# Four pairs of k-tiles by seven products, quarters on GpSimd's queue, and a transposition inside SBUF, in a hybrid decoder block

## The chip, the cores and the metric

The kernel runs on one core of a Trainium2 chip. The metric is the device time of one execution in microseconds, as a median over runs; three runs of the kernel before are shown. Engines: PE multiplies matrices and writes to PSUM, DVE (VectorE) and ACT (ScalarE) work elementwise, POOL (GpSimd) does little here but issue DMAs, SP (SyncE) only issues DMAs. Each engine takes its own instructions in order and waits for others by semaphores.

## The reference, cut to what matters

```python
D_MODEL, SEQ, D_FF = 2048, 256, 5632

def swiglu(x, w_gu, w_down):
    gate, up = jnp.split(x @ w_gu, 2, axis=-1)
    return (jax.nn.silu(gate) * up) @ w_down

def reference(x, p, ...):
    h = x
    h = h + 0.5 * swiglu(rms_norm(h, ffn1_norm), ffn1_w_gu, ffn1_w_down)
    h = h + hybrid_mixer(rms_norm(h, mix_norm), ...)      # w_in, DeltaNet + stick-breaking, w_out
    h = h + 0.5 * swiglu(rms_norm(h, ffn2_norm), ffn2_w_gu, ffn2_w_down)
    gate = jax.nn.sigmoid(rms_norm(h, ple_norm) @ ple_w_gate)
    h = h + gate * (p @ ple_w_proj)
    return rms_norm(h, final_norm)
```

Everything is float32. x has 256 rows and 2048 columns. The change is in the two feed-forward networks (FFN1 and FFN2) and, a little, in the last stage with the gate.

## The kernel before, in words

**Three products for one.** A float32 operand is cut into a high part (type fp32r) and the rest (also fp32r): x = xh + xl, w = wh + wl. A product is xh·wh + xh·wl + xl·wh, three matmuls, each with a stationary 128x128 tile of activations and a moving 128x512 tile of weights. For weights the cut is made on chip. `weight_pair` (L62) takes two k-tiles (128x1024 elements, a *pair*): SP loads them into `raw` (4 buffers, L64), ACT casts `whi` (L72), DVE subtracts `wlo` (L73); `whi` and `wlo` have 3 buffers each. One pair used as it is (*plain*) serves both halves of the 256 rows: 2 k-tiles x 2 halves x 3 = 12 matmuls (L480 to L482).

**Seven products for eight.** A *group* works on two blocks of 512 columns (b = 0, 1) at once and holds four banks of PSUM (two halves of rows x two blocks). For its first `NS` pairs of k-tiles it uses Strassen's scheme in Winograd's form: pair g is a 2x2 block matrix on either side (two k-tiles by two halves of rows; two k-tiles by two blocks of columns), and seven products of sums stand for eight. NS is 3 in the gate-and-up groups, and `NS_DOWN` is 3 or 2 in the down groups. The sums of weights are made from four *quarters* (k-tile j, block b) of NS x 512 columns: tiles `R`, four tags, loaded in `Group.load` (L270). `all_sums` (L276) yields seven sums in the order (0,0), (0,0), (0,0), (0,1), (1,0), (0,0), (1,1): each is the quarter as it stands then, cast on ACT to `shi` (L284) and subtracted on DVE to `slo` (L285), 2 buffers each. After the first sum DVE adds a quarter to another (L289) and GpSimd issues a load from DRAM that adds to a quarter (L293); after the second DVE adds once more; after the third another accumulating load. `product(i)` (L306) does 3 x NS matmuls for sum i; after products 2 and 3 DVE adds banks to banks (L324), by way of a copy on ACT (L323).

**Sums of activations.** `halves` (L393) makes the four sums on the other side, `Sh` and `Sl`: it adds high and low parts (L405), makes four sums (L412), casts (L413) and subtracts (L414), two pairs at a time.

**Stages.** Each FFN has 11 gate-and-up (gu) groups in three parts of 3, 4 and 4, and after each part two down (dn) groups of its hidden blocks. FFN1 starts with two gu groups without sums, FFN2 with one. When the last plain pair of a gu group is through, `down_input` (L433) multiplies silu(gate) by up (L435) and transposes the 256x512 result: DVE transposes 32x32 blocks (L167), SP writes them to DRAM (L171) and reads them back in another order (L181; the helper is `transposed`), then ACT and DVE cut them into `hTh` and `hTl` (L443, L444). `halves` for the dn groups runs at the start of a part's last gu group, `halves` for the next part's gu groups at the start of its second dn group.

**Order.** `plan` (L333) writes the order by hand: between the plain pairs of a group stand the seven products of the next one (*seventh*), from place `first` on, one after each plain pair. The quarters of the group after that are issued on SP from the fifth of these places on. `next_weights` keeps two to three pairs and up to two sums prepared ahead. Side work (transposes, `halves`, the mixer's chains) stands in generators in `lanes`; one step of each lane follows each plain pair. The list so written is then put in its final order on each engine by the program's scheduler, so rows of different kinds may change places.

**Elsewhere.** The mixer (stage between the FFNs) and the last stage use plain pairs alone, through `accumulate`. The last stage multiplies by `w_pg` and, in `embed`, by `w_pp`.

Of the kernel before, what the change touches and what calls it, by code (L numbers as in the profile page):

```python
# [10 lines left out]
F32 = mybir.dt.float32  # L11
# [18 lines left out]
NS = 3  # L30
NS_DOWN = tuple(3 if i1 - i0 == 4 else 2 for i0, i1 in PARTS)
# [10 lines left out]
def block_kernel(ctx, tc, a, out):  # L42
# [156 lines left out]
    def norm_block(nT, which, j, tmp):  # L199

        if j < 3:
            lanes.add(0, norm_block_behind(nT, which, j, tmp))
            return
# [39 lines left out]
    class Group:  # L243
# [24 lines left out]
        def load(self, j, b):  # L268

            self.raw[j, b] = raw = current[0].tile([P, NS, NB], F32, tag=f"R{j}{b}", name="R")[:, 0:self.ns]  # L270
            nc.sync.dma_start(out=raw, in_=self.quarters[b][j])
# [61 lines left out]
    def plan(n):  # L333
# [24 lines left out]
        made = []  # L358
        for i, group in enumerate(groups):
# [3 lines left out]
            at, loads = [], {}  # L363
# [25 lines left out]
    for nb in range(3):  # L389
        order += [("pair", a["w_pp"][nb])] + [("pair", a["w_pg"][nb][g]) for g in range(KD // 2)]  # L390
    order.append(("pair", a["w_pp"][3]))

    def halves(kind, his, los, ns, wait=0):  # L393
# [5 lines left out]
        sh = fp.tile([P, 4, NS, P], F32R, tag="Sh", name="Sh")  # L399
        sl = fp.tile([P, 4, NS, P], F32R, tag="Sl", name="Sl")  # L400
        for g0 in range(0, ns, 2):
            n = min(2, ns - g0)
            hi, lo = his[g0 // 2], los[g0 // 2]
            x = fp.tile([P, 2, 4, P], F32, tag="tT", name="tT").rearrange("p t q y -> p (t q y)")[:, 0:2 * n * T]
            nc.vector.tensor_tensor(out=x, in0=hi[:, 0:2 * n].bitcast(F32).rearrange("p k x -> p (k x)"),  # L405
                                    in1=lo[:, 0:2 * n].bitcast(F32).rearrange("p k x -> p (k x)"), op=ALU.add)
            x = x.rearrange("p (g j t y) -> p g j t y", g=n, j=2, t=2)
            a11, a12, a21, a22 = (x[:, :, j, t, :] for t in range(2) for j in range(2))
            s = fp.tile([P, 4, 2, P], F32, tag="S", name="S")[:, :, 0:n]
            for o, y, z, op in ((0, a21, a22, ALU.subtract), (1, s[:, 0], a11, ALU.subtract),  # L410
                                (2, a21, a11, ALU.subtract), (3, s[:, 1], a12, ALU.add)):
                nc.vector.tensor_tensor(out=s[:, o], in0=y, in1=z, op=op)  # L412
            nc.scalar.copy(sh[:, :, g0:g0 + n], s)  # L413
            nc.vector.tensor_tensor(out=sl[:, :, g0:g0 + n], in0=s, in1=sh[:, :, g0:g0 + n], op=ALU.subtract)  # L414
            yield

        def side(i, g):
            if i in (0, 4, 5):
                k, t = 2 * (g % 2) + (i > 0), i // 5
                c = slice(t * P, (t + 1) * P)  # L420
                return his[g // 2][:, k, c], los[g // 2][:, k, c]
            x = {1: 0, 2: 1, 3: 2, 6: 3}[i]
            return sh[:, x, g, :], sl[:, x, g, :]

        sides[kind] = side

    def ffn(n, nT, r, scale, next_norm, stat):
        xs = picker(*nT)
        late = callable(r)
        with tc.tile_pool(name="ffn", bufs=1) as fp:  # L430
            hTh, hTl = [], []

            def down_input(u, sil, th, tl):  # L433
# [4 lines left out]
                tT = fp.tile([P, 2, 4, P], F32, tag="tT", name="tT")  # L438
                yield from transposed(lambda t: sil[:, t, :], tT)
                for t in range(2):  # L440
                    hi, lo = (x[:, :, t * P:(t + 1) * P].rearrange("p j (q y) -> p q j y", q=4) for x in (th, tl))
                    tv = tT[:, t].rearrange("p q (j y) -> p q j y", j=4)
# [12 lines left out]
            for group, todo in ffn_plan[n]:  # L455
# [11 lines left out]
                for kind, one in todo:  # L467
# [19 lines left out]
                    if dn:  # L487
# [7 lines left out]
                        if group.last:  # L495
                            norm_block(nxt, next_norm, nb, lambda: fp.tile([P, 2, 4, P], F32, tag="tT", name="tT"))
                            lanes.advance(0)
# [3 lines left out]
                    else:  # L501
# [8 lines left out]
                        gen = down_input(outs, sil, th, tl)  # L510
# [58 lines left out]

    pp = ctx.enter_context(tc.tile_pool(name="pp", bufs=1))  # L570
    pT = act.tile([P, 2, T], F32, tag="nat", name="pT", bufs=4)
    nc.sync.dma_start(out=pT, in_=a["pT"])
    ph = pp.tile([P, 2, T], F32R, tag="ph", name="ph")
    pl = pp.tile([P, 2, T], F32R, tag="pl", name="pl")
    nc.scalar.copy(ph, pT)
    nc.vector.tensor_tensor(out=pl, in0=pT, in1=ph, op=ALU.subtract)
# [4 lines left out]
    with tc.tile_pool(name="fin", bufs=1) as fp:  # L581
        fg = fp.tile([P, D], F32, tag="fg", name="fg")
        nc.scalar.dma_start(out=fg, in_=a["final_norm"].broadcast_to([P, D]))
        stat = new_stat()
# [18 lines left out]
        for nb in range(3):  # L603
            e = embed(nb)
            gt = [mm_ps("gt") for _ in range(2)]
            accumulate(gt, xs, KD)
            for t in range(2):
# [671 lines left out]
```

## Time and profile before

| what | value |
|---|---|
| median of three runs | 1961.52 us (1959.1 to 1963.86) |
| the profiled execution | 1958.5 us, of which the span is 1956.8 us |
| granted TensorE clock | 0.998 |
| VectorE busy | 1536.0 us, 78% |
| ScalarE busy | 1153.7 us, 59% |
| GpSimd busy | 83.9 us, 4% |
| DMA | 468.28 MB, mean 239 GB/s |

The span runs from the first to the last instruction; the profiled execution's time is 1.7 us longer. FFN1 lies between 8 and 697 us, the mixer between 698 and 1159 us, FFN2 up to 1847 us, the last stage after that. A stretch of 40 us is about one group. Matmul ends are modelled, so a matmul's listed length (389 ns) is more than the distance from one to the next; the pace is read from a stretch of known count. A row of groups reads: line, engine, operation, out<-in, shape, count, then busy time and mean ns of one, then the engine's idle time just before them and what ended it.

### The profile page before, as it was taken

What the parts mean: (1) busy time and instruction counts of PE and PEld (TensorE: products, weight loads), DVE (VectorE), ACT (ScalarE), POOL (GpSimd) and SP (SyncE); (2) the same over time, 40 slices, a digit from 0 to 9 for tenths busy, and PEclk for the clock granted to TensorE, in tenths of its full rate; (3) what the DMA queues carried; (4) which work ended last, traced back from release to release, by engine and by line L of the source; (5) the groups of instructions that cost most, each with busy time, mean ns of one, the idle gap of its engine ahead of it and who ended that gap; (6) DMA issues with size and microseconds to landing.
All of it is one profiled execution on the core that took longest, in us unless ns stands there. A gap on an engine that the chain in (4) does not pass through costs nothing.

```text
span 1956.8 us, 24735 instructions
## 1 busy us (share of the span) xinstructions
PE 1939.7 (99%) x8945; PEld 1606.5 (82%) x8945; DVE 1536.0 (78%) x1771; ACT 1153.7 (59%) x1402; POOL 83.9 (4%) x108
## 2 busy tenths in 40 slices
PE   9999999999999999999999999999999999999998
PEld 7887888888888888878788888888888888888887
DVE  6889778897788766797856678888879887798755
ACT  7655656566565567664555465665566555665554
POOL 0000000000000000010100000000000000000000
PEclk9999999999999999999999999999999999999999
DMA  8988888888888765556555788887888878887764
GB/s 316 296 238 255 265 275 243 261 257 260 264 254 256 222 209 165 174 169 213 178 195 160 243 289 243 253 270 242 250 265 281 281 223 247 261 271 239 236 207 147
DMA packets 164379, 468.28 MB, mean 239 GB/s; under 512 B 20641, under 2 KB 59553, under 8 KB 164129
## 3 DMA queue, kind: packets, MB, share of 16 engines
q1 hardware_dynamic: 154176, 418.57, 62.1%
q0 software_dynamic: 8928, 46.67, 13.6%
q8 instruction: 70, 1.15, 0.2%
q10 hardware_dynamic: 1152, 1.47, 0.2%
q14 instruction: 53, 0.43, 0.1%
HBM read 444.62 MB, written 22.02 MB: 238 GB/s over the span
## 4 chain that ended last, share of the span: by engine, by line
PE 90%; DVE 5%; issue 3%; DMA 1%; ACT 1%; POOL 0%; SPq 0%; ACTq 0%; POOLq 0%; DVEq 0%
PE u L481 6%; PE u L482 6%; PE u L480 5%; PE g L480 5%; PE g L482 5%; PE g L481 5%; PE d L480 5%; PE d L482 5%; PE d L481 5%; PE pj L108 3%; PE pj L109 3%; PE pj L107 3%; PE g L316 3%; PE g L318 3%; PE g L317 3%
## 5 line engine op out<-in xcount | busy, mean ns | idle before, releaser
L72 ACT CAST whi<-raw 128x1024 fp32r<-128x1024 f32 (+1 forms) x531 | 557.0, 1051 | 525.3 <-PE d L482 113.6
L73 DVE TENSOR_TENSOR wlo<-raw,whi 128x1024 fp32r<-128x1024 f32 (+1 forms) x531 | 643.2, 1216 | 217.9 <-ACT whi L72 212.5
L285 DVE TENSOR_TENSOR slo<-R,shi 128x1536 fp32r<-128x1536 f32 (+1 forms) x217 | 365.6, 1686 | 125.1 <-ACT shi L284 123.5
L284 ACT CAST shi<-R 128x1536 fp32r<-128x1536 f32 (+1 forms) x217 | 309.7, 1428 | 158.6 <-PE g L318 50.6
L481 PE MATMUL u<-wlo,nTh 128*128 128x512 f32 x476 | 185.3, 389 | 0.2 <-DVE wlo L73 0.2
L481 PE MATMUL g<-wlo,nTh 128*128 128x512 f32 x476 | 185.4, 390 | 0.0
L482 PE MATMUL g<-whi,nTl 128*128 128x512 f32 x476 | 185.3, 389 | 0.0
L482 PE MATMUL u<-whi,nTl 128*128 128x512 f32 x476 | 185.2, 389 | 0.0
L480 PE MATMUL u<-whi,nTh 128*128 128x512 f32 x476 | 184.9, 389 | 0.0
L480 PE MATMUL g<-whi,nTh 128*128 128x512 f32 x476 | 184.3, 389 | 0.3 <-ACT whi L72 0.3
L107 PE MATMUL pj<-whi,nTh 128*128 128x512 f32 x448 | 179.6, 401 | 0.0
L108 PE MATMUL pj<-wlo,nTh 128*128 128x512 f32 x448 | 175.3, 391 | 2.2 <-DVE wlo L73 2.2
L109 PE MATMUL pj<-whi,nTl 128*128 128x512 f32 x448 | 174.9, 390 | 0.0
L481 PE MATMUL d<-wlo,hTh 128*128 128x512 f32 x448 | 174.3, 389 | 0.0
L480 PE MATMUL d<-whi,hTh 128*128 128x512 f32 x448 | 174.3, 389 | 0.0
L482 PE MATMUL d<-whi,hTl 128*128 128x512 f32 x448 | 174.3, 389 | 0.0
L289 DVE TENSOR_TENSOR R<-R 128x1536 f32<-128x1536 f32 (+1 forms) x62 | 104.4, 1684 | 0.9
L481 PEld LDWEIGHTS u<-wlo,nTh 128*128 128x128 f32 x476 | 89.3, 188 | 19.1 <-DVE wlo L73 0.7
L481 PEld LDWEIGHTS g<-wlo,nTh 128*128 128x128 f32 x476 | 89.4, 188 | 19.0 <-DVE wlo L73 0.4
L480 PEld LDWEIGHTS g<-whi,nTh 128*128 128x128 f32 x476 | 89.3, 188 | 18.9 <-ACT whi L72 0.5
L482 PEld LDWEIGHTS u<-whi,nTl 128*128 128x128 f32 x476 | 89.4, 188 | 18.6
L480 PEld LDWEIGHTS u<-whi,nTh 128*128 128x128 f32 x476 | 89.3, 188 | 18.6
(304 smaller groups left out, 3223.8 us busy)
## 6 DMA issues: line engine op xcount, KB each, us to landing
raw<-in_w_gu SPq DMA_DIRECT2D x237, 512.0 KB, 5.5
raw<-in_w_down SPq DMA_DIRECT2D x112, 512.0 KB, 5.2
raw<-in_w_in SPq DMA_DIRECT2D x112, 512.0 KB, 3.5
R<-in_w_gu2q SPq DMA_DIRECT2D x40, 768.0 KB, 5.9
R<-in_w_gu1q SPq DMA_DIRECT2D x36, 768.0 KB, 5.9
scr<-tb SPq DMA_DIRECT2D x74, 256.0 KB, 4.8
raw<-in_w_out SPq DMA_DIRECT2D x32, 512.0 KB, 4.6
raw<-in_w_pg SPq DMA_DIRECT2D x32, 512.0 KB, 4.1
```

The lines of the kernel that those rows point to most:

```text
L72: nc.scalar.copy(hi[:, j, :], raw[:, j, :])
L73: nc.vector.tensor_tensor(out=lo[:, j, :], in0=raw[:, j, :], in1=hi[:, j, :], op=ALU.subtract)
L107: nc.tensor.matmul(outs[t], xh[:, c], whi[:, j, :], start=st, stop=False)
L108: nc.tensor.matmul(outs[t], xh[:, c], wlo[:, j, :], start=False, stop=False)
L109: nc.tensor.matmul(outs[t], xl[:, c], whi[:, j, :], start=False, stop=sp)
L284: nc.scalar.copy(hi, w)
L285: nc.vector.tensor_tensor(out=lo, in0=w, in1=hi, op=ALU.subtract)
L289: nc.vector.tensor_tensor(out=self.raw[x], in0=self.raw[x], in1=self.raw[y], op=ALU.add)
L316: nc.tensor.matmul(out, xh, whi[:, g, :], start=st, stop=False, skip_group_check=True)
L480: nc.tensor.matmul(out, xh[:, c], whi[:, j, :], start=st, stop=False, skip_group_check=True)
L481: nc.tensor.matmul(out, xh[:, c], wlo[:, j, :], start=False, stop=False, skip_group_check=True)
L482: nc.tensor.matmul(out, xl[:, c], whi[:, j, :], start=False, stop=sp, skip_group_check=True)
```

## The change

Seven parts:

- `NS` goes from 3 to 4, and `NS_DOWN` from 3 to 4 in the parts of four blocks. The quarters, `shi`, `slo`, `Sh` and `Sl` grow by a third.
- `raw` has three buffers in place of four.
- The quarters of all but the first group with sums are issued by GpSimd, in the order (0,0), (0,1), (1,1), (1,0); each takes the buffer that the group before frees next (`home`). The fourth is carried over into the next group.
- The seven products follow each other from place 1, 2 or 8 on, one after each plain pair.
- `down_input` no longer goes through DRAM: sixteen DMAs, each 32 partitions by 1 KB, carry the blocks from SBUF to SBUF; the high and low parts are made three or four steps later.
- `halves` makes its four sums in place, in the tile `sil` which it shares with `down_input`.
- Norm blocks alternate between two lanes and two tiles; `embed` comes behind the eight pairs of `w_pg`, and p is cut in the last stage.

```diff
-NS = 3
-NS_DOWN = tuple(3 if i1 - i0 == 4 else 2 for i0, i1 in PARTS)
+NS = 4
+NS_DOWN = tuple(4 if i1 - i0 == 4 else 2 for i0, i1 in PARTS)
...
-        raw = wp.tile([P, 2, NB], F32, tag="raw", name="raw", bufs=4)
+        raw = wp.tile([P, 2, NB], F32, tag="raw", name="raw", bufs=3)
...
-            self.raw[j, b] = raw = current[0].tile([P, NS, NB], F32, tag=f"R{j}{b}", name="R")[:, 0:self.ns]
-            nc.sync.dma_start(out=raw, in_=self.quarters[b][j])
-
-        def loads(self):
-            return [("load", lambda j=j, b=b: self.load(j, b)) for j, b in ((0, 1), (1, 0), (0, 0), (1, 1))]
+            self.raw[j, b] = raw = current[0].tile([P, NS, NB], F32, tag=self.home[j, b], name="R")[:, 0:self.ns]
+            self.queue.dma_start(out=raw, in_=self.quarters[b][j])
+
+        def loads(self, last=None):
+            free = [last.home[q] for q in ((0, 1), (1, 0), (0, 0), (1, 1))] if last else ["R0", "R1", "R2", "R3"]
+            self.queue = nc.gpsimd if last else nc.sync
+            use = (0, 0), (0, 1), (1, 1), (1, 0)
+            self.home = dict(zip(use, free))
+            return [("load", lambda q=q: self.load(*q)) for q in use]
...
-                first = 2 if group.ns else 8
-                at = [first + j * (n_plain - 1 - first) // 7 for j in range(7)]
+                first = 8 if not group.ns else 1 if group.kind == follower.kind else 2
+                at = [min(first + j, n_plain - 1) for j in range(7)]
...
-                    for x, one in zip((5, 6, 7, 7), after.loads()):
-                        loads.setdefault(at[x] if x < 7 else min(at[6] + 1, n_plain - 1), []).append(one)
+                    *three, last = after.loads(follower)
+                    for x, one in zip((4, 5, 6), three):
+                        loads.setdefault(at[x], []).append(one)
+                    carried = [last]
...
-        order += [("pair", a["w_pp"][nb])] + [("pair", a["w_pg"][nb][g]) for g in range(KD // 2)]
+        order += [("pair", a["w_pg"][nb][g]) for g in range(KD // 2)] + [("pair", a["w_pp"][nb])]
...
+            x = fp.tile([P, 2 * NB], F32, tag="sil", name="S")[:, 0:n * NB]
...
+            for o, y, z, op in ((a22, a21, a22, ALU.subtract), (a21, a21, a11, ALU.subtract),
+                                (a11, a22, a11, ALU.subtract), (a12, a11, a12, ALU.add)):
+                nc.vector.tensor_tensor(out=o, in0=y, in1=z, op=op)
...
-                tT = fp.tile([P, 2, 4, P], F32, tag="tT", name="tT")
-                yield from transposed(lambda t: sil[:, t, :], tT)
+                tb = fp.tile([P, 4, 2, P], F32, tag="tb", name="tb")
+                for t in range(2):
+                    nc.vector.transpose(tb[:, :, t].rearrange("p c (j x) -> p c j x", j=4),
+                                        sil[:, t, :].rearrange("p (j c x) -> p c j x", j=4, c=4))
+                yield
+                tT = fp.tile([P, 4, 2, P], F32, tag="tT", name="tT")
+                for c in range(4):
+                    for q in range(4):
+                        nc.sync.dma_start(out=tT[32 * c:32 * c + 32, q], in_=tb[32 * q:32 * q + 32, c])
+                    if c == 1 and wait > 3:
+                        yield
+                for _ in range(wait):
+                    yield
```

Three places show how the order moves. The first is DVE at the start of a gu group in the second part of FFN1; `slo` is a sum, `R` a quarter, `tb` the transposed blocks. Before:

```order
L285 TENSOR_TENSOR slo_2142<-R_2061,shi_2141 128x1536
L289 TENSOR_TENSOR R_2061<-R_2061,R_2020 128x1536
L73 TENSOR_TENSOR wlo_2106<-raw_2104,whi_2105 128x1024
L285 TENSOR_TENSOR slo_2172<-R_2061,shi_2171 128x1536
L435 SCALAR_TENSOR_TENSOR sil_1961<-u0_1623,rstd2_517,sil_1961 128x512
L435 SCALAR_TENSOR_TENSOR sil_1961<-u1_1624,rstd2_517,sil_1961 128x512
L73 TENSOR_TENSOR wlo_2137<-raw_2135,whi_2136 128x1024
L167 STREAM_TRANSPOSE tb_2161<-sil_1961 128x512
L167 STREAM_TRANSPOSE tb_2162<-sil_1961 128x512
L73 TENSOR_TENSOR wlo_2167<-raw_2165,whi_2166 128x1024
L289 TENSOR_TENSOR R_2061<-R_2061,R_2063 128x1536
```

The same place in the change:

```order
L291 TENSOR_TENSOR slo_2118<-R_1999,shi_2117 128x2048
L445 SCALAR_TENSOR_TENSOR sil_1974<-u0_1633,rstd2_515,sil_1974 128x512
L295 TENSOR_TENSOR R_1999<-R_1999,R_2041 128x2048
L445 SCALAR_TENSOR_TENSOR sil_1974<-u1_1634,rstd2_515,sil_1974 128x512
L73 TENSOR_TENSOR wlo_2141<-raw_2139,whi_2140 128x1024
L451 STREAM_TRANSPOSE tb_2174<-sil_1974 128x4x128
L291 TENSOR_TENSOR slo_2158<-R_1999,shi_2157 128x2048
L451 STREAM_TRANSPOSE tb_2174<-sil_1974 128x4x128
L295 TENSOR_TENSOR R_1999<-R_1999,R_2077 128x2048
```

The two additions of quarters now have one plain pair's `wlo` between them, where three stood, and both they and the sums are a third longer.

The second place is PE in the last gu group of the same part, where the products of the first dn group (banks d) stand between plain pairs (banks g and u). Before:

```order
L316 MATMUL d0_2878<-shi_2826,Sh_2809 128x512
L317 MATMUL d0_2878<-slo_2827,Sh_2809 128x512
L318 MATMUL d0_2878<-shi_2826,Sl_2810 128x512
L480 MATMUL g0_2534<-whi_2855,nTh_102 128x512
L481 MATMUL g0_2534<-wlo_2856,nTh_102 128x512
L482 MATMUL g0_2534<-whi_2855,nTl_106 128x512
L480 MATMUL g1_2535<-whi_2855,nTh_102 128x512
```

The same place in the change:

```order
L504 MATMUL u1_2522<-whi_2853,nTl_105 128x512
L322 MATMUL d0_2880<-shi_2818,Sh_2802 128x512
L323 MATMUL d0_2880<-slo_2819,Sh_2802 128x512
L322 MATMUL d1_2879<-shi_2894,Sh_2802 128x512
L502 MATMUL u0_2521<-whi_2900,nTh_101 128x512
L503 MATMUL u0_2521<-wlo_2901,nTh_101 128x512
L323 MATMUL d1_2879<-slo_2895,Sh_2802 128x512
L504 MATMUL u0_2521<-whi_2900,nTl_105 128x512
```

Before, a product was finished before the next pair began; now two products and a plain pair alternate matmul by matmul.

The third place is the issue of quarters. Before, SP issued them (L271) between the plain pairs:

```order
L69 DMA raw_2077<-in_w_gu1 128x1024
L271 DMA R_2020<-in_w_gu1q 128x1536
L69 DMA raw_2104<-in_w_gu1 128x1024
L271 DMA R_2053<-in_w_gu1q 128x1536
L69 DMA raw_2135<-in_w_gu1 128x1024
L271 DMA R_2061<-in_w_gu1q 128x1536
L69 DMA raw_2165<-in_w_gu1 128x1024
L271 DMA R_2063<-in_w_gu1q 128x1536
```

In the change the same quarters stand on POOL, ahead of the accumulating loads (L299) of their group:

```order
L271 DMA R_1999<-in_w_gu1q 128x2048
L271 DMA R_2041<-in_w_gu1q 128x2048
L271 DMA R_2077<-in_w_gu1q 128x2048
L271 DMA R_2085<-in_w_gu1q 128x2048
L299 DMA R_2041<-in_w_gu1q 128x2048
L299 DMA R_1999<-in_w_gu1q 128x2048
```

SP keeps the plain pairs alone, and gets the sixteen small transfers of each gu group.

More of the change, by code (lines that the diff above doesn't have):

```diff
@@ L197, in norm_block_behind, with norm_block @@
                 yield
-    def norm_block(nT, which, j, tmp):
+    def norm_block(nT, which, j, tmp, lane=0):
         if j < 3:
-            lanes.add(0, norm_block_behind(nT, which, j, tmp))
+            lanes.add(lane, norm_block_behind(nT, which, j, tmp))
             return
@@ L398, in halves @@
         fp = current[0]
[L399 to L415, printed above, removed]
+        sh = fp.tile([P, NS, 2, 2, P], F32R, tag="Sh", name="Sh")
+        sl = fp.tile([P, NS, 2, 2, P], F32R, tag="Sl", name="Sl")
         def side(i, g):
@@ L495, in ffn @@
                         if group.last:
[L496 to L497 removed]
+                            norm_block(nxt, next_norm, nb, lambda x=("tT", "sil")[nb % 2]:
+                                       fp.tile([P, 2, 4, P], F32, tag=x, name="tT"), nb % 2)
+                            lanes.advance(nb % 2)
                     elif b == 0:
@@ L509, in ffn @@
                         hTl.append(tl)
-                        gen = down_input(outs, sil, th, tl)
+                        gen = down_input(outs, sil, th, tl, 3 if len(hTh) == PARTS[group.part][1] else 4)
                         next(gen)
@@ L583, in block_kernel, with split_p @@
         nc.scalar.dma_start(out=fg, in_=a["final_norm"].broadcast_to([P, D]))
+        ph = fp.tile([P, 2, T], F32R, tag="ph", name="ph")
+        pl = fp.tile([P, 2, T], F32R, tag="pl", name="pl")
+        def split_p():
+            pT = act.tile([P, 2, T], F32, tag="nat", name="pT", bufs=4)
+            nc.sync.dma_start(out=pT, in_=a["pT"])
+            for _ in range(3):
+                yield
+            nc.scalar.copy(ph, pT)
+            nc.vector.tensor_tensor(out=pl, in0=pT, in1=ph, op=ALU.subtract)
+        lanes.add(2, split_p())
         stat = new_stat()
```

32 lines of the change are left out of this document (18 added, 14 removed).

## The prediction

> **What bounds the kernel now.** I read the page's head first, then PE's waits, then stretches of some 40 us, then DVE's groups.
>
> ```profile
> span 1956.8 us, 24735 instructions
> PE 1939.7 (99%) x8945; PEld 1606.5 (82%) x8945; DVE 1536.0 (78%) x1771; ACT 1153.7 (59%) x1402; POOL 83.9 (4%) x108
> ...
> PE pj L108 <- DVE wlo L73: 2.2, 4, 1.1
> PE u L316 <- ACT Sh L413: 1.3, 2, 0.9
> PE vp L1011 <- DVE R L1032: 1.2, 1, 1.2
> ```
>
> PE is busy for all but 17 us of the span, and its three longest waits in the whole program add up to 4.7 us. So PE is the bound: fewer matmuls shorten the kernel, and nothing else can, except that a new wait on PE lengthens it. What a matmul is worth, and how near DVE is to becoming the bound, is read from stretches. The columns are length, busy time and count of PE, PEld, DVE, ACT and POOL, then clock and DMA.
>
> ```profile
> 338.00:464.20 126.20, 126.20 (x558) 104.45 (x558) 109.34 (x107) 75.08 (x73) 5.26 (x6) 1.00 0.84 256
> ...
> 155.00:192.00 37.00, 36.09 (x158) 29.16 (x157) 34.65 (x41) 22.23 (x25) 1.75 (x2) 1.00 0.81 256
> ...
> 1305.00:1342.00 37.00, 36.58 (x160) 29.54 (x159) 35.13 (x41) 22.76 (x25) 1.73 (x2) 1.00 0.85 270
> ```
>
> The first row spans three groups of FFN1 (a part's last gu group and its two dn groups): PE never pauses, and 126.20 us / 557 steps from start to start = 226.6 ns per matmul. DVE is busy for 87% of it. The other two rows are the tightest places of the program: DVE stands at 94% and 95%, and PE loses 0.91 and 0.42 us in 37.
>
> **The change, part by part. Matmuls.** A pair in plain form costs 24 matmuls for both blocks, by seven products 21. One more pair goes over in 9 + 10 gu groups and in 8 dn groups of the parts of four: 27 x 3 = 81 matmuls, x 226.6 ns = **-18.3 us**. PE has no other idle time to give back.
>
> **DVE.** Its durations by shape (busy us, mean ns):
>
> ```profile
> L73 DVE TENSOR_TENSOR wlo<-raw,whi 128x1024 fp32r<-128x1024 f32 x529 | 641.8, 1218 | 216.4 <-ACT whi L72 211.2 <-DMA tT<-scr 1.5 <-DMA raw<-in_w_down 1.5
> L285 DVE TENSOR_TENSOR slo<-R,shi 128x1536 fp32r<-128x1536 f32 x189 | 331.6, 1755 | 121.5 <-ACT shi L284 121.1
> L289 DVE TENSOR_TENSOR R<-R 128x1536 f32<-128x1536 f32 x54 | 94.7, 1753 | 0.8
> ...
> L412 DVE TENSOR_TENSOR S<-tT 128x256 f32<-128x256 f32 x24 | 9.4, 416 | 0.0
> ...
> L412 DVE TENSOR_TENSOR S<-tT 128x128 f32<-128x128 f32 x20 | 5.0, 283 | 0.0
> ...
> L405 DVE TENSOR_TENSOR tT<-nTh,nTl 128x512 f32<-128x512 f32 x6 | 4.1, 684 | 0.0
> ```
>
> From 1024 to 1536 elements is +0.537 us, so 2048 elements are an estimated 2.29 us. Per group: seven `slo` and two additions, 9 x 0.537 = +4.8, less two `wlo`, -2.4: **+2.4 us** of DVE in 0.68 us less of PE. One call of `halves` was 2 x (1.22 + 0.68) + 4 x 0.416 + 4 x 0.283 = 6.6 and becomes 4 x 1.22 + 8 x 0.416 = 8.2: +1.6. In the stretch from 338 to 464 us that makes 109.3 + 3 x 2.4 + 2 x 1.6 = 119.7 us of DVE in 126.2 - 9 x 0.2266 = 124.2 us: 96%, with 4.5 us left. At the head of a group two slots each hold `wlo`, `slo` and an addition, 1.22 + 2 x 2.29 = 5.8 us, against 24 matmuls, 5.44 us; the two pairs that PE has in hand cover 0.7 us.  Whether 4.5 us is enough depends on how much of DVE's idle time there is forced:
>
> ```profile
> DVE slo L285 <- ACT shi L284: 12.1, 14, 1.9
> DVE wlo L73 <- ACT whi L72: 4.1, 7, 1.1
> ...
> ACT whi L72 <- PE d L482: 20.2, 18, 1.7
> ACT shi L284 <- PE d L318: 6.0, 6, 1.0
> ...
> ACT shi L284 <- DVE R L289: 3.5, 2, 2.1
> ...
> ACT hTh L443 <- DMA tT<-scr: 0.2, 1, 0.2
> ```
>
> DVE idles 16.2 us there behind ACT, but ACT mostly waits for PE to free a buffer, which is slack, not need. ACT's waits for others than PE (six rows, from the 3.5 to the 0.2 us shown) are 8.9 us. So DVE's forced idle time lies between 0 and 8.9 us, and PE's new wait per stretch between 0 and 8.9 - 4.5 = 4.4. There are four such stretches (parts of four, two per FFN): 0 to 18 us. I take 1.5 us each, **+6**, by the 37 us rows: 0.4 to 0.9 us at 94 to 95%, and a stretch is three times as long. The order shown for PE there, two products and a pair alternating, is what I expect to fill such gaps with other work.
>
> **Quarters and accumulating loads.**
>
> ```profile
> R<-in_w_gu2q SPq DMA_DIRECT2D x40, 768.0 KB, 5.9
> ...
> R<-in_w_gu2q POOLq DMA_DIRECT2D x20, 768.0 KB, 8.3
> ...
> L293 POOL DMA_DIRECT2D R<-in_w_gu1q x1: 875/875/875, 559.4 to 559.4; - x1
> ...
> DMA to landing us min/median/max: 10.6/10.6/10.6
> ...
> 571.11 1.49 ACT L284 CAST shi<-R 128x1536 fp32r<-128x1536 f32 x1
> ...
> DMA to landing us min/median/max: 7.3/7.3/7.3
> ```
>
> The quarters have over four slots of 5.44 us between issue and use, so a plain load from GpSimd may take twice the 5.9 us and cost nothing; issuing takes POOL 0.9 us. The tight one is the second accumulating load, needed by the sixth sum: issued at 559.4, landed after 10.6 us, used at 571.1, so 1.1 us to spare of 11.7. One issued at 435.0, with quarters of SP hardly beside it, landed in 7.3 us (the last row). A megabyte is 4/3: 9.7 to 14.1 us, against 11.7 + 2 slots x 0.68 = 13.1. The quarters now stand behind it on the same queue instead of beside it on SP's, so I take the lower end: **0**, upper end 1.0 us in each of 27 groups. [...]
>
> **Transposition and SP.** One DMA issue in a row costs SP 0.64 us, and a 32 KB transfer (here one to DRAM, the nearest there is) lands in 2.4 us:
>
> ```profile
> 348.49 2.54 SPq L181 DMA_DIRECT2D tT<-scr  x4
> ...
> sc<-dec SPq DMA_DIRECT2D x8, 32.0 KB, 2.4
> ```
>
> Sixteen issues are 10.2 us, and the last lands some 12.6 us after the first; three or four steps of 5.44 us (16 or 22 us) stand before the use. The plain pair's load queued behind them comes 10.2 us late; with landing 5.5, cast 1.05 and `wlo` 1.22 that is 18 us, against three slots for the buffers of `raw` and two for the pairs in hand, 27 us. So 0, hidden by pairs in hand; without the two pairs it would be 18 - 16.3 = 1.7 us in each of 22 gated blocks. The round trip through DRAM that goes was hidden too: no wait of PE names it.
>
> **Three buffers of `raw`, first quarters.**
>
> ```profile
> SPq L69 <- DVE wlo L73: 900.8, 394, 8.2
> ...
> raw<-in_w_gu SPq DMA_DIRECT2D x237, 512.0 KB, 5.5
> ...
> raw<-in_w_in SPq DMA_DIRECT2D x112, 512.0 KB, 3.5
> ...
> 1158.49 2.05 SPq L271 DMA_DIRECT2D R<-in_w_gu2q  x4
> ...
> DMA to landing us min/median/max: 5.5/8.2/10.3
> ...
> DMA to landing us min/median/max: 3.9/6.6/9.2
> ```
>
> SP waits for a free `raw` 394 times: loads run as far ahead as buffers allow. With three, a cycle of landing, cast and `wlo` must fit three pairs, 36 x 0.2266 = 8.2 us: in the mixer 3.5 + 2.3 = 5.8 fits, in the plain groups 5.5 + 2.3 = 7.8 just fits. At FFN2's start it is tighter: the plain load behind the four first quarters landed after 9.2 us (third landing row, maximum), and the quarters themselves after 5.5 to 10.3, 1.6 us apiece; at 4/3 the load lands about 2 us later, 11.3, and 13.6 with its cuts, against six pairs less 2.5 us = 13.8. I take **+2** for both FFN starts (0 to 6). Products drawn forward fill part of it. The mixer I take at 0, upper end 3. Last stage, lanes and `halves` in place change no count on PE; `halves` and silu sharing one tile is inside the stretches' price.
>
> **Sum.** From 1958.5 us of the profiled execution: -18.3 + 6 + 2 = -10.3, 1948.2. The median of the runs shown is 3.0 us above that execution: 1951.
>
> **Rivals.** *Full gain*: no new waits, 1961.5 - 18.3 = 1943. For it: scheduling already holds PE's waits at 95% DVE under 1 us; against: 96% over 124 us is more than any row shows. *DVE binds in the stretches*: forced idle time at its upper end, 18 + 2 us of waits, 1963, no gain. For it the 5.8 us slots and ACT's waits for DVE; against, that most idle time is behind PE. *Late accumulating load* (the other side): ACT stands at the sixth sum's cast until the megabyte has landed, and what is queued behind it, `whi` of the next pairs and with it `wlo` on DVE, comes as late, with no DVE slack to catch up. At 14.1 us of landing against 13.1 that is 1.0 us x 27 = 27 on top of the forecast's 8: 1961.5 - 18.3 + 35 = 1978. It decides from 13.1 us on. *GpSimd kept from issuing by DVE*: if an issue had to wait out a DVE instruction, up to 2.3 us, the middle landing of 11.9 becomes 14.2, 1.1 us x 27 = 30 more, 1981. Against it: the issue takes 875 ns in both rows above, under a DVE busy for 87%. [...]
>
> **Chances.** Forecast 0.50, full gain 0.22, DVE binds 0.15, late load 0.11, GpSimd held 0.02. A measurement here tells about 0.2%, 3.9 us. Faster is forecast and full gain, 0.72; within 0.2% is DVE binds, 0.15; slower 0.13. The range runs from 1942, the full gain, to 1964, just above DVE binds, and leaves the 0.13 out.
>
> **What would show it.** Right: 81 matmuls fewer at 226.6 ns; `slo` at 2.3 us; DVE at 94 to 97% in the third and fourth gu groups and the dn groups; PE's waits around 12 to 15 us, on `Sh`, `slo` and `wlo`, at part ends and FFN starts. Wrong: ACT waiting for DMA R before many `shi` (late load), PE waiting on `wlo` behind late `raw` inside gu groups (SP's sixteen issues or three buffers), or PE waits above 18 us.

## The result, and the profile after

The changed kernel takes 2109.28 us (median of 4 runs, 2104.58 to 2120.98) against 1960.94 us before: ratio 1.076, 95% interval 1.072 to 1.081. It is slower by 148 us. By stage (to the last `h` of each, in the two profiled executions) FFN1 went from 698.1 to 770.4 us, the mixer from 461.1 to 463.4, FFN2 from 688.9 to 759.0, the last stage from 108.7 to 110.1. All but 4 us of the loss is in the FFNs, where the gated blocks and the groups with seven products are.

The head of the page of the changed kernel, and its chain of work that ended last:

```profile
span 2102.9 us, 24549 instructions
PE 1991.4 (95%) x8864; PEld 1619.1 (77%) x8864; DVE 1613.2 (77%) x1717; ACT 1174.1 (56%) x1348; POOL 147.9 (7%) x224
...
PE 43%; DMA 18%; DVE 17%; issue 10%; SPq 6%; ACT 6%; POOL 0%; ACTq 0%; POOLq 0%; DVEq 0%
DMA raw<-in_w_gu 7%; SPq L457 6%; DVE slo L291 4%; DMA tT<-tb 4%; DVE wlo L73 4%; DMA raw<-in_w_down 4%; ACT shi L290 3%; PE pj L108 3%; PE pj L107 3%; PE pj L109 3%; PE g L323 2%; DVE R L295 2%; PE g L324 2%; PE g L322 2%; PE d L503 2%
```

The 81 matmuls are gone as forecast (8864 for 8945), and still PE's busy time rose by 51.7 us. PE now idles for 2102.9 - 1991.4 = 111.5 us, before 17.1. Before, the chain ran 90% through PE; now SP's issue of the blocks' transfers (L457), their landing (`tT<-tb`) and the raw loads stand in it. The waits that name the cause, for PE, ACT, DVE and SP (total us, times, longest):

```profile
PE d L322 <- ACT Sh L433: 19.4, 7, 4.8
PE d L322 <- ACT shi L290: 18.5, 13, 3.3
PE g L323 <- DVE slo L291: 16.9, 12, 1.8
PE g L322 <- ACT shi L290: 16.8, 8, 3.0
...
ACT hTh L465 <- DMA tT<-tb: 101.2, 18, 8.8
ACT whi L72 <- DMA raw<-in_w_gu: 52.6, 45, 5.5
ACT whi L72 <- DMA raw<-in_w_down: 45.2, 24, 6.5
...
DVE hTl L466 <- ACT hTh L465: 58.1, 13, 8.5
...
SPq L457 <- DVE tb L451: 92.4, 22, 11.6
SPq L69 <- DMA raw<-in_w_gu: 92.1, 32, 7.4
```

PE waits for cuts that ACT and DVE make too late; ACT itself stands idle ahead of `hTh`, 101.2 us, mostly 5 to 9 us at a time. One gated block shows how. First SP in the timeline from 276 to 302 us, then ACT from 276 to 310 us (start, length, instruction; in brackets the idle time before it and what ended it):

```profile
280.44 0.33 SPq L69 DMA_DIRECT2D raw<-in_w_gu  x1
283.86 10.81 SPq L457 DMA_DIRECT2D tT<-tb  x16
294.76 2.53 SPq L69 DMA_DIRECT2D raw<-in_w_gu  x3
```

```profile
290.61 1.91 ACT L290 CAST shi<-R 128x2048 fp32r<-128x2048 f32 x1 [1.11 <-PE u L324]
292.61 1.37 ACT L471 ACTIVATE sil<-g,rstd 128x512 f32<-128x512 f32 x2
299.89 1.14 ACT L465 CAST hTh<-tT 128x512 fp32r<-128x512 f32 x2 [5.91 <-DMA tT<-tb]
301.40 1.05 ACT L72 CAST whi<-raw 128x1024 fp32r<-128x1024 f32 x1 [0.37 <-DMA raw<-in_w_gu]
302.36 1.90 ACT L290 CAST shi<-R 128x2048 fp32r<-128x2048 f32 x1
...
306.45 1.05 ACT L72 CAST whi<-raw 128x1024 fp32r<-128x1024 f32 x1 [1.72 <-DMA raw<-in_w_gu]
```

The sixteen issues hold SP from 283.86 to 294.7. No raw load goes out between 280.4 and 294.8, and the next `whi` is cast at 301.4. ACT arrives at `hTh` at 294.0 and stands there for 5.91 us, in front of a weight and a sum that PE needs soon. What PE does then is in the windows from 298 us on (length; busy time of PE, PEld, DVE, ACT, POOL; granted clock; DMA):

```profile
298.00:304.00 6.00, 6.00 (x28) 4.73 (x26) 3.13 (x4) 3.74 (x4) 0.00 (x0) 1.00 0.92 353
304.00:306.00 2.00, 0.63 (x2) 0.19 (x1) 1.71 (x1) 0.73 (x2) 0.00 (x0) 1.00 1.02 408
...
308.00:310.00 2.00, 2.00 (x6) 1.58 (x5) 1.97 (x3) 2.00 (x2) 0.00 (x0) 0.50 0.86 248
310.00:312.00 2.00, 2.00 (x8) 1.60 (x7) 1.70 (x1) 2.00 (x3) 0.00 (x0) 0.81 0.99 410
312.00:314.00 2.00, 2.00 (x10) 1.66 (x9) 2.00 (x3) 1.22 (x2) 0.54 (x1) 1.00 0.32 131
```

PE pauses between 304.8 and 306.6, for the `slo` of the sum that ACT could cast only at 302.36. Then its clock is granted at 0.50, and it needs 2 us for 6 matmuls where some 9 went before: the pause is paid a second time, as slow work that counts as busy. Over the whole span the mean clock fell from 0.998 to 0.971. So the 146.1 us between the two spans are +94.4 idle time of PE, +57.1 clock (0.029 x 2102.9 less 0.002 x 1956.8) and -18.3 matmuls, 133.2 in all; 12.9 us are left unassigned. The 57.1 us are an estimate, and a high one: the mean clock counts a slow stretch whole, with the pauses inside it.

### The profile page after: what moved, and what is told of

The parts are those of the page before. It is cut to its first block, busy times and chain, and to the rows that moved or that the text cites. A ratio compares the mean times of both kernels' runs of the same rounds, so it can differ in the third digit from the quotient of the medians.

```text
span 2102.9 us, 24549 instructions
## 1 busy us (share of the span) xinstructions
PE 1991.4 (95%) x8864; PEld 1619.1 (77%) x8864; DVE 1613.2 (77%) x1717; ACT 1174.1 (56%) x1348; POOL 147.9 (7%) x224
## 4 chain that ended last, share of the span: by engine, by line
PE 43%; DMA 18%; DVE 17%; issue 10%; SPq 6%; ACT 6%; POOL 0%; ACTq 0%; POOLq 0%; DVEq 0%
DMA raw<-in_w_gu 7%; SPq L457 6%; DVE slo L291 4%; DMA tT<-tb 4%; DVE wlo L73 4%; DMA raw<-in_w_down 4%; ACT shi L290 3%; PE pj L108 3%; PE pj L107 3%; PE pj L109 3%; PE g L323 2%; DVE R L295 2%; PE g L324 2%; PE g L322 2%; PE d L503 2%
## 5 line engine op out<-in xcount | busy, mean ns | idle before, releaser
L72 ACT CAST whi<-raw 128x1024 fp32r<-128x1024 f32 (+1 forms) x477 | 498.6, 1049 | 435.3 <-PE pj L109 102.6
L73 DVE TENSOR_TENSOR wlo<-raw,whi 128x1024 fp32r<-128x1024 f32 (+1 forms) x477 | 577.4, 1216 | 194.1 <-ACT whi L72 193.0
L291 DVE TENSOR_TENSOR slo<-R,shi 128x2048 fp32r<-128x2048 f32 (+1 forms) x217 | 465.1, 2148 | 101.7 <-ACT shi L290 99.6
L290 ACT CAST shi<-R 128x2048 fp32r<-128x2048 f32 (+1 forms) x217 | 389.8, 1801 | 202.0 <-DVE R L295 79.6
L295 DVE TENSOR_TENSOR R<-R 128x2048 f32<-128x2048 f32 (+1 forms) x62 | 132.7, 2140 | 0.2
L322 PE MATMUL g<-shi,nTh 128*128 128x512 f32 x228 | 96.0, 421 | 17.0 <-ACT shi L290 16.8
L323 PE MATMUL g<-slo,nTh 128*128 128x512 f32 x228 | 96.8, 425 | 15.5 <-DVE slo L291 15.5
L108 PEld LDWEIGHTS pj<-wlo,nTh 128*128 128x128 f32 x448 | 84.3, 188 | 22.4 <-DVE wlo L73 6.5
L322 PE MATMUL d<-shi,Sh 128*128 128x512 f32 x160 | 71.3, 445 | 30.5 <-ACT Sh L433 19.4
L109 PEld LDWEIGHTS pj<-whi,nTl 128*128 128x128 f32 x448 | 84.1, 188 | 17.6
```

What stands on the lines that cost most here:

```text
L72: nc.scalar.copy(hi[:, j, :], raw[:, j, :])
L73: nc.vector.tensor_tensor(out=lo[:, j, :], in0=raw[:, j, :], in1=hi[:, j, :], op=ALU.subtract)
L108: nc.tensor.matmul(outs[t], xh[:, c], wlo[:, j, :], start=False, stop=False)
L109: nc.tensor.matmul(outs[t], xl[:, c], whi[:, j, :], start=False, stop=sp)
L290: nc.scalar.copy(hi, w)
L291: nc.vector.tensor_tensor(out=lo, in0=w, in1=hi, op=ALU.subtract)
```

## The experiments

Theory T (later split into S and A): the sixteen small transfers from SBUF to SBUF do it. S is the part by SP, whose issues keep raw loads back; A is the part by ACT, which stands in order ahead of `hTh`. The rivals: D (VectorE can't carry the sums of four pairs), B (three raw buffers) and Q (quarters on GpSimd's queue). All runs, with the median, the ratio to before and its interval; of the profiled execution PE's idle time (span less busy), the mean clock, and ACT's idle time ahead of `hTh` (whatever ended it) and ahead of `whi` (where a load of `raw` ended it):

| run | us | ratio (95%) | PE idle | clock | hTh | whi |
|---|---|---|---|---|---|---|
| before | 1961 | | 17.1 | 0.998 | 2.3 | 14.2 |
| changed | 2109 | 1.076 (1.072-1.081) | 111.5 | 0.971 | 112.8 | 132.5 |
| e6_raw3_only | 1975 | 1.007 (1.005-1.009) | 28.4 | 0.998 | 4.7 | 165.3 |
| e2_sbuf_only | 2065 | 1.053 (1.052-1.055) | 93.5 | 0.983 | 131.5 | 57.5 |
| e10_sbuf_pool | 2025 | 1.032 (1.029-1.034) | 64.4 | 0.991 | 106.5 | 32.6 |
| f2_sbuf_behind2 | 2029 | 1.035 (1.032-1.037) | 57.5 | 0.990 | 12.7 | 105.3 |
| e9_sbuf_wait2 | 2067 | 1.053 (1.050-1.056) | 97.7 | 0.983 | 131.5 | 61.2 |
| g1_sbuf_pool_behind2 | 2000 | 1.020 (1.018-1.021) | 40.3 | 0.992 | 9.2 | 12.4 |
| e5_dram_raw4 | 2037 | 1.039 (1.036-1.042) | 77.9 | 0.983 | 115.0 | 25.6 |
| e7_wait2 | 2046 | 1.042 (1.038-1.047) | 86.9 | 0.981 | 119.5 | 29.3 |
| e8_sp_quarters_raw4 | 2012 | 1.025 (1.021-1.028) | 61.3 | 0.990 | 71.3 | 31.5 |
| g3_poolq_behind2 | 2020 | 1.031 (1.028-1.033) | 64.9 | 0.989 | 34.0 | 79.6 |
| f1_spq_behind2 | 1981 | 1.010 (1.008-1.012) | 39.8 | 0.994 | 13.5 | 55.8 |
| f4_spq_ns3 | 1971 | 1.004 (1.003-1.006) | 22.4 | 0.999 | 22.6 | 28.1 |
| g2_spq_behind2_down3 | 1967 | 1.003 (1.002-1.004) | 27.4 | 0.997 | 4.8 | 84.3 |
| e1_dram | 2086 | 1.063 (1.061-1.065) | 112.9 | 0.977 | 120.1 | 103.0 |
| e3_sp_quarters | 2097 | 1.069 (1.067-1.071) | 108.9 | 0.973 | 114.8 | 137.2 |
| h1_after_pool_spq | 2058 | 1.048 (1.042-1.053) | 86.5 | 0.983 | 94.5 | 103.7 |
| g4_after_ns3 | 2085 | 1.063 (1.061-1.065) | 92.8 | 0.983 | 119.6 | 176.0 |
| f3_after_behind1 | 2124 | 1.083 (1.081-1.085) | 129.7 | 0.968 | 0 | 258.0 |

### One part of the change alone, or undone

The transposition taken back in the changed kernel (e1), put alone into the kernel of before (e2), the fourth raw buffer given back beside e1 (e5), and three buffers alone (e6).

```diff
-                for c in range(4):
-                    for q in range(4):
-                        nc.sync.dma_start(out=tT[32 * c:32 * c + 32, q], in_=tb[32 * q:32 * q + 32, c])
...
+                yield from transposed(lambda t: sil[:, t, :], tT)
...
-        raw = wp.tile([P, 2, NB], F32, tag="raw", name="raw", bufs=3)
+        raw = wp.tile([P, 2, NB], F32, tag="raw", name="raw", bufs=4)
```

The first edit is e1's, both are e5's; on the kernel of before e2 makes the first the other way round, and e6 the second.

> The changed kernel with the gated blocks' transposition taken back to the way of before (through DRAM, two transfers out and two in); seven products for four pairs, three raw buffers and quarters from GpSimd's queue stay. Theory T (transposition): the 16 transfers from SBUF to SBUF hold SP for about 10 us per gated block, ScalarE stands in order behind their landing, and the raw loads behind them come too late for three buffers; with them gone the time falls from 2109 us to 1943 to 1975 us, and the low granted clock after TensorE's pauses goes too (mean above 0.99). Rival D (VectorE cannot keep up with the sums of four pairs): still 2080 us or more. Rival B (three raw buffers alone starve TensorE): still 2060 us or more. Rival Q (quarters and accumulating loads on one queue): still 2080 us or more.

> The kernel of before with one part of the change: the gated blocks' transposition from SBUF to SBUF (VectorE transposes 32 x 32 pieces, 16 transfers from SP). Three pairs by seven products, four raw buffers, quarters from SP stay. Theory T: 22 gated blocks at some 5 us lost each, half of it paid again by the low clock, give 2020 to 2110 us. If T needs the missing fourth buffer too (T and B together): 1970 to 2020 us. Rivals D, B and Q: within 15 us of 1961 us.

> As the run with the transposition through DRAM, and with four raw buffers again: only the seven products for four pairs, the order of their sums and the quarters' queue are left of the change. Theory T: 1940 to 1955 us (81 matmul groups of 226.6 ns gone is 18 us under 1961 us). Rival B: the same 1940 to 1955 us, but then the run with three buffers is 100 us slower than this. Rivals D and Q: 2080 us or more.

> The kernel of before with three raw buffers in place of four, nothing else. Theory T: 1961 to 1975 us, as SP is not held up there. Rival B: 2030 us or more. Rivals D and Q: 1961 us as before.

T is half right. Alone, the transposition costs 104 us (e2), as T said. But with it gone the changed kernel still takes 2086 us (e1), where T said 1975 at most and D, B and Q are all within their bounds; with the fourth buffer too it takes 2037 (e5), which none of them said. What is left of the change there costs 76 us, where 18 were to be gained. ACT stands ahead of `hTh` as long without the small transfers (120.1 us in e1, 115.0 in e5) as with them (112.8), and only 2.3 us in the kernel of before. So beside the rest of the change the way through DRAM isn't hidden either. B alone costs 14 us (e6): ACT stands 165 us ahead of `whi` there, yet PE loses only 11 us of it, as most is hidden by the pairs in hand. In company the third buffer is worth more, 49 us between e1 and e5. The losses are not a sum of parts; that every part draws on the same two or three pairs in hand would explain it, but is argued, not shown.

### SP or ScalarE: what makes the transposition dear

Two ways to undo one half of it: issue the sixteen transfers from GpSimd (S), or put `hTh` later on ACT (A). The first try at the second, e9 on e2 and e7 on e5, wrote the copies two steps later and nothing else.

```diff
-                        nc.sync.dma_start(out=tT[32 * c:32 * c + 32, q], in_=tb[32 * q:32 * q + 32, c])
+                        nc.gpsimd.dma_start(out=tT[32 * c:32 * c + 32, q], in_=tb[32 * q:32 * q + 32, c])
...
-                        gen = down_input(outs, sil, th, tl, 3 if len(hTh) == PARTS[group.part][1] else 4)
+                        gen = down_input(outs, sil, th, tl, 3 if len(hTh) == PARTS[group.part][1] else 6)
```

The first edit is e10's, the second e9's; e7 adds two steps at the end of `transposed`.

> The kernel of before with the transposition from SBUF to SBUF (2065 us), with hTh two steps later in blocks that are not the last of their part. Theory A: ScalarE's idle time ahead of hTh falls from 6.2 us a block to under 2 us, and the time to 1965 to 2000 us. Theory S (SP's 16 issues, 10 us, keep the raw loads behind them, and that alone starves TensorE): 2040 us or more.

> The kernel of before with the transposition from SBUF to SBUF (2065 us), its 16 transfers issued from GpSimd in place of SP. GpSimd takes 0.87 us for an issue, so the last goes out some 14 us after the first, beside 10 us on SP. Theory S: SP is free for the raw loads, and the time falls to 1965 to 2000 us. Theory A: the landing comes later still, ScalarE stands longer ahead of hTh (8 us a block or more), and the time is 2060 to 2150 us.

> The run with the transposition through DRAM and four raw buffers (2037 us), with one edit: in blocks that are not the last of their part, ScalarE's hTh copies stand two steps (two weight pairs) later in the program. In that run ScalarE stood idle 5.4 us ahead of hTh in a mean gated block (22 blocks, 118 us; before: 1.2 us a block). Theory A (ScalarE, in order, stands behind the landing at hTh, and the halved sums and weights behind it come late for TensorE): the idle time falls under 2 us in the blocks edited and the time to 1950 to 1995 us. Theory D (VectorE's queue is full with four pairs, so everything on it comes late): 2020 us or more. Theory Q (the 1 MB quarters on GpSimd's queue slow the other transfers): 2020 us or more, the idle time only moves elsewhere.

e9 decides nothing: the scheduler gave PE, ACT, DVE and SP the same rows in the same order as in e2, so it is a repeat (2067 us against 2065). e7 (2046 against 2037 us) left `hTh` in its place as well (5 of its 44 copies moved, by one row): ACT's 119.5 us ahead of it compare with e5's 115.0. The place of `hTh` is the scheduler's, and later writing doesn't move it. With SP free, e10 gave back 40 us, though ACT still stood 106.5 us; its 2025 us lie between what S and A said.

So `hTh` and `hTl` were tied behind the latest weight cut that is written ahead of them, an edge of order alone, on top of the later place:

```diff
+            latest[0] = nc.scalar.copy(hi[:, j, :], raw[:, j, :])
+            latest[1] = nc.vector.tensor_tensor(out=lo[:, j, :], in0=raw[:, j, :], in1=hi[:, j, :], op=ALU.subtract)
...
+                    with tc.issue_after(latest[0].ins), tc.issue_after(latest[1].ins):
                         nc.scalar.copy(hi, tv)
                         nc.vector.tensor_tensor(out=lo, in0=tv, in1=hi, op=ALU.subtract)
```

> The kernel of before with the transposition from SBUF to SBUF (2065 us), hTh and hTl held two steps later in the same way. Theory A: 1961 to 1985 us. Theory S: 2030 us or more.

> The kernel of before with the transposition from SBUF to SBUF (2065 us), its 16 transfers from GpSimd (alone: 2025 us) and hTh held two steps later on ScalarE (alone: 2029 us). If SP's issues and ScalarE's standing are the whole cost of the transposition (theory S + A): 1961 to 1980 us. If a third cause is left (the 16 small transfers themselves, or VectorE's hTl): 1995 us or more.

> The changed kernel with one edit: ScalarE's hTh and VectorE's hTl are held behind the weight copies that stand ahead of them in the program as written, and one step later in blocks that are not the last of a part; in the final order hTh then comes four to five copies (whi, shi) later on ScalarE. (An earlier try to put them later without holding them there left ScalarE's final order as it was.) ScalarE stood 5.2 us a block ahead of hTh in the changed kernel. Theory A (ScalarE standing ahead of hTh is what makes the weights and sums late): the standing falls under 1.5 us in most blocks and the time from 2109 to 1960 to 2030 us. Theory S (SP's 16 issues hold the raw loads, three buffers): 2070 us or more with the standing gone, and ScalarE then waits for raw instead. Theory D (VectorE): 2080 us or more.

ACT's waits in e2, and then in f2:

```profile
ACT hTh L454 <- DMA tT<-tb: 114.9, 19, 8.4
...
ACT whi L72 <- DMA raw<-in_w_gu: 31.7, 15, 4.9
```

```profile
ACT whi L74 <- DMA raw<-in_w_gu: 92.5, 34, 6.4
...
ACT hTh L457 <- DMA tT<-tb: 12.7, 2, 6.5
```

The wait ahead of `hTh` goes, and of the 119 us that go there by the table 48 come back ahead of `whi`, since SP still sends the raw loads late. That is S, laid bare: 36 us gained, 68 left, 1 us under the 2030 us of S. Both halves undone (g1) leave neither wait, and 2000 us: 65 of the 104 us are S and A. A remainder of 39 us was expected only if a third cause exists. In g1 PE's longest waits are 8.6 us each for `shi` and for `Sh` at the first sums of the down groups; whether they belong to the transposition or to the place given to `hTh` was not tried. In the changed kernel itself the hold alone (f3) gained nothing, 2124 us: all 112.8 us ahead of `hTh` went and ACT's waits for raw doubled from 132.5 to 258.0, as S said. There, by this run, late raw loads are the bound, and moving ACT's wait doesn't help.

### Four pairs and the quarters' queue

All these have the transposition through DRAM and four buffers. Quarters from SP (e8); the same with `hTh` held later (f1); that with GpSimd's queue again (g3); e8 with three pairs (f4); f1 with three pairs in the down groups alone (g2).

```diff
-            self.queue = nc.gpsimd if last else nc.sync
+            self.queue = nc.sync
...
-NS = 4
-NS_DOWN = tuple(4 if i1 - i0 == 4 else 2 for i0, i1 in PARTS)
+NS = 3
+NS_DOWN = tuple(3 if i1 - i0 == 4 else 2 for i0, i1 in PARTS)
```

The queue is edited in all but g3, `NS` in f4 alone, `NS_DOWN` in f4 and g2.

> The run with the transposition through DRAM and four raw buffers (2037 us), with the quarters issued from SP in place of GpSimd. There the last transfer of a gated block landed 7.6 us after its issue in the mean, before 3.7 us. Theory Q: the landing falls to 5 us or less and the time to 1950 to 1990 us. Theories A and D: landing and time hardly move, 2020 us or more; if quarters now hold up the raw loads in SP's order, above 2045 us.

> Transposition through DRAM, four raw buffers, quarters from SP (2012 us), hTh and hTl held two steps later. Theory A: the standing of 3.7 us a block falls under 1 us, the pauses of TensorE in the gu groups (17 us at shi) go, and the time is 1945 to 1975 us. Theory D: pauses behind shi and slo stay, 2000 us or more.

> Transposition through DRAM, four raw buffers, quarters from SP (2012 us), with three pairs by seven products in place of four; what is left of the change is the order of the loads and sums and the halves made in place. Theory D (four pairs ask more of VectorE and ScalarE within the group than they can give): 1958 to 1972 us, the time of before. Theory O (the new order of sums and loads, or the halves in place, does it whatever the number of pairs): 1995 us or more. Theory A says the same as D if the standing ahead of hTh goes with the third pair (under 1.5 us a block).

> As the run that took 1981 us, with the quarters issued from GpSimd as in the change. Without hTh held later, GpSimd's issue cost 24 us (2037 against 2012). If that cost came only by ScalarE standing for late transfers (theory A): 1975 to 1990 us. If the quarters on that queue take time from raw and the sums by themselves (theory Q): 2000 us or more.

> Transposition through DRAM, four raw buffers, quarters from SP, hTh held two steps later (1981 us), with four pairs by seven products in the gate-and-up groups alone; the down groups keep three (two in the first part). Of 28.9 us of TensorE's idle time there, 17.2 us stand ahead of the first sums of the down groups, where VectorE had worked without a gap for 29 us. Theory D: that idle time falls under 5 us, which with its low clock outweighs the 24 matmuls (5.4 us) that come back: 1955 to 1970 us. Otherwise (the idle time stays): 1980 to 1990 us.

With everything else repaired but ACT's standing, the fourth pair takes the time from 1971 to 2012 us, a loss of 42 us instead of a gain of 18 (f4, e8). The new order of sums and loads and the sums made in place (theory O, 1995 us or more) are in f4 too, which ends 10 us above before. Holding `hTh` later gives back 32 us (f1): so much was A. It ends 20 us above before, between what A and D said. The rest of D is in f1's windows at the end of a part, where DVE makes the down groups' `halves` beside the sums (columns as above):

```profile
340.00:369.00 29.00, 29.00 (x127) 23.38 (x126) 28.58 (x30) 15.13 (x15) 1.76 (x2) 1.00 0.83 235
369.00:376.00 7.00, 4.15 (x17) 2.68 (x16) 5.89 (x7) 5.52 (x7) 0.00 (x0) 0.98 0.76 288
```

DVE is busy for 28.58 of 29 us, 99%, and as it ends PE lacks the down group's first sums and idles for 2.85 us in 7. In all, f1's PE waits 17.2 us for those `shi`; with three pairs in the down groups that wait is gone, and the run takes 14 us less though 24 matmuls came back (g2):

```profile
PE d L326 <- ACT shi L294: 17.2, 12, 1.9
```

```profile
PE d L326 <- ACT Sh L437: 5.9, 7, 1.9
```

The quarters on GpSimd's queue cost 24 us with `hTh` in its old place (e5, e8) and 40 with it held (g3, f1), so their price does not come only by the `hTh` that could be held. Q's own sign, sooner landing, isn't it: the last transfer of a gated block's transposition lands 7.6 us after its issue in e5 and 7.0 in e8 (mean of 22), where Q said 5 or less. A 128 KB transfer of it (`tT<-scr`) lands in 7.5 us with a quarter in flight (median of 76) and in 3.5 without (64, most of them in other stages) in e5, and in 7.7 (74) and 3.4 (66) in e8. Nor are the quarters themselves much later: the plain ones of the gate-and-up groups land in 7.7 us from GpSimd (68 in e5, without the accumulating loads) and in 6.7 from SP (76 in e8). What differs is how long SP's raw loads wait for what the profile puts down to the landing of an earlier raw load, in e5 and then in e8:

```profile
SPq L69 <- DMA raw<-in_w_gu: 73.5, 15, 9.8
```

```profile
SPq L69 <- DMA raw<-in_w_gu: 8.2, 6, 3.9
```

With `hTh` held it is 81.4 us in g3 and 17.6 in f1. So the price comes with late raw loads; why they are late beside GpSimd's quarters, and whether it is the queue or the moment at which the quarters go out, stays open.

### In the changed kernel itself

Three pairs in place of four (g4); quarters from SP (e3); that and the sixteen transfers from GpSimd (h1). The edits are those shown above.

> The changed kernel with three pairs by seven products in place of four; transposition from SBUF to SBUF, three raw buffers and quarters from GpSimd stay. Theory S + A (the transposition does most of it, whatever the number of pairs): 2050 to 2110 us. Theory D (four pairs are what VectorE can't carry, and the transposition only hurts beside them): 2010 us or less.

> The changed kernel (2109 us) with the quarters issued from SP in place of GpSimd, all else as changed. Theory Q (the quarters' queue costs 24 to 39 us, as in the two pairs of runs with the transposition through DRAM): 2065 to 2090 us. If SP is what is short in the changed kernel (theory S), four more issues a group on it cost time: 2105 us or more.

> As the run before it, and the 16 transfers of the transposition issued from GpSimd in place of SP. Theory S: 40 us or more below the run before it, 2000 to 2045 us, and SP's raw loads no longer wait behind the transposed blocks. If ScalarE's standing alone matters: within 15 us of it.

Three pairs take 2085 us: the loss does not need the fourth pair, which adds 24 us to it here. The quarters' queue is worth only 13 us here, between the two expectations, and the sixteen issues off SP another 39; S said 40 or more, but 2045 us at most, and it is 2058. Single parts undone (e1, e3, g4) end between 2085 and 2097 us. The changed kernel with four raw buffers and nothing else undone wasn't run. None of the runs beats the kernel of before; the nearest, g2, is 0.3% above it with 57 matmuls fewer.

## Why the prediction was wrong, point by point

**Matmuls, -18.3: right.** 81 are gone, and undisturbed ones still follow each other at 227 ns.

**Transposition and SP, 0: this step failed.** It read: "Sixteen issues are 10.2 us, and the last lands some 12.6 us after the first; three or four steps of 5.44 us (16 or 22 us) stand before the use", and "So 0, hidden by pairs in hand". The issues were sized well, 11.0 us from first to last in the mean of 22 blocks; the last landed 4.3 us after that, 15.3 from the first for 12.6. Wrong was what they were held against. First, the three or four steps are those of the list as written. In the final order ACT comes to `hTh` 10.5 us after SP's first issue (mean of 22 blocks), before even the forecast's 12.6, and stands there, 112.8 us in 22 blocks (before: 2.3), with `shi` and `whi` of the next products behind it. Second, SP was counted from its first issue; it had by then stood still for `tb` as well, 92.4 us in 22 blocks, and the raw loads were late by both. Third, late raw was held against the full 27 us of pairs in hand and late `hTh` against the steps alone, each as if the other were not there; f2 shows that with one wait gone the other grows. Alone the part costs 104 us, of which S and A were shown to be 65; the cause of the other 39 is open. The prediction's sentence on what would show it wrong, PE waiting on `wlo` behind late raw, named the right place (SP) but the wrong row: the waits stand on `shi`, `slo` and `Sh`. Its other sign, PE waits above 18 us, came true: PE's idle time rose by 94 us.

**DVE, +6 (0 to 18): mis-sized.** Durations were right (`slo` of 2048 elements 2286 ns, estimated 2290). But four pairs cost 42 us where a gain of 18 was due (f4, e8): 60 us, ten times the term, of which holding `hTh` takes 32 away (f1). The estimate took DVE's busy time over 124 us, 96%. What decides is the 29 us at a part's end where it is 99% busy, and a second effect that the sum over a stretch can't show: DVE's transposes come later (from product to transposed block 6.2 us in e8, 2.1 in f4), so the landing and, it seems, ACT's wait ahead of `hTh` do too.

**Quarters, 0: wrong, by 13 to 40 us.** The accumulating loads landed sooner than the forecast's 9.7 us (8.7 us for 1 MB in the median of the 38 in gate-and-up groups, 11.7 at most), and ACT stood ahead of `shi` for them for 8.4 us in all, in 8 places; the rival of a late load, 27 us of PE, did not come. The price came with raw loads that were late beside them (e5 and g3), which the step did not look at.

**Three buffers, +2: 14 us alone (e6)**, 5.2 us in FFN1 and 10.4 in FFN2, and more in company. The mixer, taken at 0 with an upper end of 3, moved by 0.6 there.

**No term at all for the clock.** Every wait was priced at its length. Some 57 of the 146 us are, by the estimate above, clock lost after pauses. The rivals ended at 1981 us in part for the same reason: each priced one wait at its length and none the two or three that meet in a gated block. GpSimd kept from issuing by DVE was not seen: in the changed kernel its issues took 540 to 895 ns in the mean of their groups, under a DVE busy for 77%.

## What to carry to other kernels

Small transfers cost their issues here: sixteen of 32 KB held SP for 11 us per block, and the raw loads behind them on that queue were late (none went out from 280.4 to 294.8 us in the block shown). Where an engine copies out what a transfer brings and takes its instructions in order, as ACT did (112.8 us ahead of `hTh`), ask what stands behind the copy in that engine's queue, not when the result is used, and check in the final order that a later place was really taken. Cover such as two pairs in hand can be spent once: add up all that is late against it, and price a long pause of a full TensorE at more than its length: in the changed kernel 94 us of new idle time came with an estimated 57 us of lost clock, while e6, with 11 us of it, kept the clock of before, 0.998.

## What the runs showed of the hardware

In the changed kernel, a pause of PE of 1.82 us (304.8 to 306.6; one of 0.18 us stood a matmul ahead of it) was followed by some 3.4 us at a granted clock of 0.50, a pause of 2.65 us (349.1 to 351.8) by a stretch of 0.50 that lasted past 358 us, with another pause of 1.53 us in it. In the changed kernel's clock record every slow stretch between 50 and 1940 us lasted 3.41 or 6.83 us. Of the pauses that began at full clock, all 13 above 2 us brought such a stretch, at the latest 2.1 us after their end, and none of the 13 between 0.5 and 1 us did. Between the two, length alone doesn't decide: a pause of 1.83 us at 152.4 us brought none.

A 32 KB transfer inside SBUF landed in 1.84 us with no quarter in flight, plain or accumulating (median of 55, in the changed kernel), and in 4.36 with one (297); 512 KB of `raw<-in_w_down` took 4.04 (25) and 6.94 us (71). The forecast's 2.4 us for the small transfer was from a quiet place.
